# Turning the gated product through VectorE blocks and DRAM instead of TensorE, in nine of eleven FFN steps

## The chip, the cores and the metric

The kernel runs on one core of one Trainium2 chip. The metric is the device time in microseconds of one execution: the median of three runs. The profile shows one further execution, with the engines PE (TensorE), DVE (VectorE), ACT (ScalarE), POOL (GpSimd) and SP (SyncE, which only issues transfers here).

## The reference, cut to what matters

The program is a chain of two transformer blocks on 256 rows of width 1024, in float32. Six times in it stands a gated feed-forward network (FFN) of inner width 2816, and it is the FFN that the change touches:

```
def swiglu_ffn(h, w1, w3, w2):
    return (jax.nn.silu(h @ w1) * (h @ w3)) @ w2
...
        h = h + FFN_RES_WEIGHT * swiglu_ffn(rmsnorm(h, ffn_norm1[i]), ffn1_w1[i], ffn1_w3[i], ffn1_w2[i])
```

Between the FFNs stand a convolution, a latent attention (mla) and a mixer with two more attentions; these are not changed. A projection of a conditioning vector, `mod = silu(c) @ w_mod + b_mod`, is worked out beside the FFNs, in pieces.

## The kernel before, in words

The 256 rows are two row tiles t = 0 and 1 of 128 rows. An FFN runs over NF = 11 steps j of 256 inner columns. The input stands transposed in `x[t]`, split into a high part `xh` and a low part `xl`; each product is three matmuls (high·high, high·low, low·high), the function `mm3`.

In a step, `load(j)` brings three units of 1 MB through SP's queue into a ring of four `raw` buffers: two for w1 and w3 (`up`), one for w2 (`down_in`). ACT casts each 128x512 piece into `whi` (line 82) and DVE makes the rest `wlo` (line 83): 12 pieces a step. `whi`/`wlo` hold 16 pieces for w1 and w3, which is two steps, and 8 for w2. `gu(j, t)` is 24 matmuls of 128x512 into a PSUM bank `wk` (four banks); `gate(j, t)` then makes SiLU on ACT (`sg`, line 340) and the gated product on DVE (`gg`, line 342). `turn(j, t)` transposes `gg` by two PE transposes against an identity (line 106) into PSUM and splits the result into `gh` (ACT, line 82) and `gl` (DVE, line 83). `down(j, t)` is 12 matmuls of `gh`, `gl` with w2 into two banks `acc`.

In the middle steps the code stands in the order load(j), gu(j,0), gu(j,1), then for each tile down(j-1,t), turn(j,t). So a step is 72 matmuls of 128x512 and four transposes. Every engine takes its instructions in one fixed order, which a scheduler writes at build time; an instruction that waits holds up all behind it on its engine. For the part where `pinned` is set, PE keeps the order of the code.

In every second middle step of the first five FFNs, three or four times in each, `mid` calls `mod_group`: two units of w_mod of 1 MB are summed with the conditioning vector in eight DVE instructions into `macc` (lines 992 and 996), two matmuls add over partitions, and a row `mrow` of 512 elements is loaded (line 1006), added to and written to DRAM.

The convolution already sends data through DRAM with POOL's transfers: `land` (line 580) issues four transfers, each of 32 partitions with 8 runs of 624 bytes.

Of the kernel before, what the change touches and what calls it, by code (L numbers as in the profile page):

```python
# [10 lines left out]
F32 = mybir.dt.float32  # L11
F32R = mybir.dt.float32r
# [7 lines left out]
P = 128  # L20
# [11 lines left out]
class Build:  # L32
# [284 lines left out]

    def ffn(self, w, finish, after, mid=None, slow=False, begun=None):
        nc, tc = self.nc, self.tc
        with tc.tile_pool(name=f"ffn{self.n}", bufs=1) as fp:  # L320
            self.fp = fp
            acc = [[self.bank(tag="acc") for _ in range(2)] for _ in range(2)]
            g, w2 = {}, {}

            u = {}

            def up(j):
                u[j] = [self.unit(w[3 * j + i]) for i in range(2)]

            def down_in(j):  # L330
                w2[j] = self.unit(w[3 * j + 2], pool=fp)

            def load(j):
                up(j)
                down_in(j)

            def gate(j, t, ps):
                sc = 1.0 if self.rs[t] is None else self.rs[t][:, :1]
                sg = self.t([P, 256], tag="sg", bufs=2, pool=fp)
                nc.scalar.activation(sg, ps[:, :256], AF.Silu, scale=sc)  # L340
                g[j, t] = self.t([P, 256], tag="gg", bufs=3, pool=fp)
                nc.vector.scalar_tensor_tensor(  # L342
                    out=g[j, t], in0=ps[:, 256:], scalar=sc, in1=sg, op0=ALU.mult, op1=ALU.mult
                )

            def gu(j, t):
                gate(j, t, self.cols(t, u[j], 512))

            def turn(j, t):
                hi = self.t([P, 2, P], F32R, tag=f"gh{t}", bufs=2, pool=fp)  # L350
                lo = self.t([P, 2, P], F32R, tag=f"gl{t}", bufs=2, pool=fp)
                self.transposed(g[j, t], 2, hi, lo)
                g[j, t] = hi, lo

            def down(j, t):
                self.rows(acc[t], g[j, t], w2[j], j == 0, j == NF - 1)

            if begun:
                u[0] = begun[0]
                for t in range(2):  # L360
                    gate(0, t, begun[1][t])
                with self.in_turn():
                    up(1)
                turn(0, 0)
                gu(1, 0)
                down_in(0)
                turn(0, 1)
                gu(1, 1)
                turn(1, 0)
                down_in(1)  # L370
            else:
                load(0)
                load(1)
                gu(0, 0)
                gu(1, 0)
                self.flush()
                turn(0, 0)
                gu(0, 1)
                turn(1, 0)
                gu(1, 1)  # L380
                turn(0, 1)
            down(0, 0)
            turn(1, 1)
            down(0, 1)
            self.pinned = False
            for j in range(2, NF - 1):
                load(j)
                gu(j, 0)
                gu(j, 1)
                if mid:  # L390
                    mid(j)
                for t in range(2):
                    down(j - 1, t)
                    turn(j, t)
            j = NF - 1
            load(j)
            gu(j, 0)
            down(j - 1, 0)
            turn(j, 0)
            ps = self.cols(1, u[j], 512, ks=range(4))  # L400
            down(j, 0)
            finish(0, acc[0])
            post = after(0)
            gate(j, 1, self.cols(1, u[j], 512, ps, range(4, 8)))
            down(j - 1, 1)
            turn(j, 1)
            if not slow:
                post()
            down(j, 1)
            finish(1, acc[1])  # L410
            self.pending.append(after(1))
            if slow:
                post()

    def out_rows(self, x, units, finish, after, mid=None):


        acc, done, post = {}, [0, 0], []

        def step(order):  # L420
            for c in order:
                if c in "pm":
                    (post[0] if c == "p" else mid)()
                    continue
                t = int(c)
                if t not in acc:
                    acc[t] = [self.bank(tag="acc") for _ in range(2)]
                i = done[t]
                z = tuple(v[:, 2 * i : 2 * i + 2] for v in x[t])
                self.rows(acc[t], z, units[i], i == 0, i == 3)  # L430
                done[t] += 1
                if i == 3:
                    finish(t, acc[t])
                    (self.pending if t else post).append(after(t))

        return step
# [544 lines left out]
    def mod_group(self, i):  # L981

        nc, a = self.nc, self.a
        part, which, cols = i // 6, i % 6 // 2, slice(i % 2 * 512, i % 2 * 512 + 512)
        acc = self.t([P, 512], tag="macc", pool=self.fp)
        for u in range(2):
            r = self.raw(a["wmod"][2 * i + u])
            for k in range(4):
                w = r[:, k * 512 : k * 512 + 512]
                s = self.cact[:, 4 * u + k : 4 * u + k + 1]  # L990
                if u == k == 0:
                    nc.vector.tensor_scalar(
                        out=acc, in0=w, scalar1=s, scalar2=None, op0=ALU.mult
                    )
                else:
                    nc.vector.scalar_tensor_tensor(  # L996
                        out=acc, in0=w, scalar=s, in1=acc, op0=ALU.mult, op1=ALU.add
                    )
        hi = self.t([P, 512], F32R, tag="mhi", pool=self.fp)
        lo = self.t([P, 512], F32R, tag="mlo", pool=self.fp)  # L1000
        self.split(hi, lo, acc)
        ps = self.bank()
        self.matmul(ps, self.onesr, hi, start=True, stop=False)
        self.matmul(ps, self.onesr, lo, start=False, stop=True)
        row = self.t([1, 512], tag="mrow", pool=self.fp)
        nc.sync.dma_start(out=row, in_=a["b_mod_2"][0:1, i * 512 : i * 512 + 512])
        nc.vector.tensor_add(row, ps[:1, :], row)
        if which == 1:
            name = ("norm_ffn1_2", "norm_mix_2", "norm_ffn2_2")[part]
            grow = self.t([P, 512], tag="junk")[:1]  # L1010
            nc.sync.dma_start(out=grow, in_=a[name][0:1, cols])
            nc.vector.scalar_tensor_tensor(
                out=row, in0=row, scalar=1.0, in1=grow,
                op0=ALU.add, op1=ALU.mult,
            )
        elif which == 2:
            nc.vector.tensor_scalar(
                out=row, in0=row, scalar1=0.5, scalar2=None, op0=ALU.mult
            )
        nc.sync.dma_start(out=self.mods[i], in_=row)  # L1020
# [553 lines left out]
```

## Time and profile before

| | |
|---|---|
| median of three runs | 1542.34 us (1540.28 to 1542.95) |
| the profiled execution, its own time | 1545.36 us |
| its span from first to last instruction | 1543.2 us |
| PE, DVE, ACT, POOL busy | 98%, 71%, 54%, 4% of the span |
| granted TensorE clock, mean | 0.994 |

Busy shares are means over all stages. The profiled execution is 3.0 us above the median of the runs and 2.2 us above its own span. Matmuls overlap in the records, so their pitch is read from their start times and not from their durations.

### The profile page before, as it was taken

To read this page: it belongs to the slowest core of one execution; us is meant where nothing else is said; L and a number is where in the kernel's file an instruction comes from. 1 tells how busy PE (TensorE), PEld (TensorE's weight loads), DVE (VectorE), ACT (ScalarE), POOL (GpSimd) and SP (SyncE) were. 2 spreads that over 40 slices of the span, in tenths; PEclk is the share of its full clock that TensorE was granted. 3 is DMA by queue.
4 is the path that set the end of the run, shared out by engine and by line. 5 is a ranking of instruction groups with operands and counts; after the bars stand their busy time and mean duration, and the time that the engine had idled before them with its cause. 6 is when DMAs were issued, how large, how long until landed. Compare 5 with 4: busy or idle time off the path is not lost.

```text
span 1543.2 us, 21250 instructions
## 1 busy us (share of the span) xinstructions
PE 1515.7 (98%) x7824; PEld 1239.0 (80%) x7824; DVE 1093.6 (71%) x2136; ACT 830.2 (54%) x1723; POOL 54.6 (4%) x84
## 2 busy tenths in 40 slices
PE   8999997999999999999999999999999999999998
PEld 6888886888888888888788888788888877878886
DVE  7977566587765887658589755888657886975552
ACT  7555454565545555546475544545545565665541
POOL 0000013000000000000000000100001100000000
PEclk9999999999999999999999999999999999999999
DMA  8886479177764676644268754487552543565530
GB/s 307 304 295 254 168 263 254 52 282 270 255 238 149 240 265 232 236 137 143 104 214 310 265 186 176 151 304 273 190 190 97 173 157 120 196 240 189 193 109 28
DMA packets 54923, 316.68 MB, mean 205 GB/s; under 512 B 9210, under 2 KB 12026, under 8 KB 19108
## 3 DMA queue, kind: packets, MB, share of 16 engines
q1 hardware_dynamic: 50596, 308.92, 55.4%
q0 software_dynamic: 2048, 5.11, 1.4%
q10 hardware_dynamic: 2176, 1.30, 0.3%
q8 instruction: 61, 1.00, 0.2%
q14 instruction: 42, 0.34, 0.1%
HBM read 312.93 MB, written 2.39 MB: 204 GB/s over the span
## 4 chain that ended last, share of the span: by engine, by line
PE 91%; DVE 4%; issue 2%; DMA 1%; POOL 1%; ACT 1%; SPq 0%; POOLq 0%; DVEq 0%; ACTq 0%
PE wk L103 52%; PE acc L103 35%; PE wk L106 4%; DVE wlo L83 1%; DMA shifted<-shift 1%; POOL sm L130 1%; DMA h<-in_x_dram 0%; DVE sm L1195 0%; DVE y L259 0%; DVE h L1038 0%; DVE y L1037 0%; ACT pb L1207 0%; DVE pb L1248 0%; DVE pb L1244 0%; DVE y L744 0%
## 5 line engine op out<-in xcount | busy, mean ns | idle before, releaser
L83 DVE TENSOR_TENSOR wlo<-raw,whi 128x512 fp32r<-128x512 f32 x996 | 652.1, 684 | 58.8 <-ACT whi L82 57.0
L82 ACT CAST whi<-raw 128x512 fp32r<-128x512 f32 x996 | 587.5, 619 | 95.0 <-DMA raw<-in_f_dram 27.7
L103 PE MATMUL wk<-whi,xh 128*128 128x512 f32 x1120 | 443.8, 396 | 0.5
L103 PE MATMUL wk<-wlo,xh 128*128 128x512 f32 x1120 | 437.5, 391 | 0.2 <-DVE wlo L83 0.2
L103 PE MATMUL wk<-whi,xl 128*128 128x512 f32 x1120 | 437.6, 391 | 0.0
L103 PEld LDWEIGHTS wk<-whi,xl 128*128 128x128 f32 x1120 | 210.8, 188 | 44.9
L103 PEld LDWEIGHTS wk<-whi,xh 128*128 128x128 f32 x1120 | 211.0, 188 | 43.5 <-ACT xh L85 1.5
L103 PEld LDWEIGHTS wk<-wlo,xh 128*128 128x128 f32 x1120 | 211.2, 189 | 42.8 <-DVE wlo L83 0.6
L103 PE MATMUL acc<-whi,gh 128*128 128x512 f32 x528 | 212.2, 402 | 1.0 <-ACT gh L82 0.9
L103 PE MATMUL acc<-whi,gl 128*128 128x512 f32 x528 | 207.3, 393 | 0.0
L103 PE MATMUL acc<-wlo,gh 128*128 128x512 f32 x528 | 206.7, 392 | 0.0
L340 ACT ACTIVATE sg<-wk,sm 128x256 f32<-128x256 f32 x88 | 41.7, 474 | 195.5 <-PE wk L103 194.1
L342 DVE SCALAR_TENSOR_TENSOR gg<-wk,sm,sg 128x256 f32<-128x256 f32 x88 | 42.4, 481 | 110.0 <-ACT sg L340 108.6
L103 PE MATMUL acc<-whi,xh 128*128 128x512 f32 (+2 forms) x304 | 117.9, 388 | 0.7 <-ACT xh L82 0.7
L103 PEld LDWEIGHTS acc<-whi,gl 128*128 128x128 f32 x528 | 99.1, 188 | 21.7
L103 PEld LDWEIGHTS acc<-whi,gh 128*128 128x128 f32 x528 | 99.3, 188 | 21.4 <-ACT gh L82 2.1
L103 PE MATMUL acc<-wlo,xh 128*128 128x512 f32 (+2 forms) x304 | 116.1, 382 | 0.0
L103 PE MATMUL acc<-whi,xl 128*128 128x512 f32 (+2 forms) x304 | 115.7, 382 | 0.0
L103 PEld LDWEIGHTS acc<-wlo,gh 128*128 128x128 f32 x528 | 99.4, 188 | 19.9
L82 ACT CAST gh<-wk 128x256 fp32r<-128x256 f32 x132 | 48.8, 370 | 120.6 <-PE wk L106 120.5
L83 DVE TENSOR_TENSOR gl<-wk,gh 128x256 fp32r<-128x256 f32 x132 | 55.4, 420 | 64.1 <-ACT gh L82 64.0
L996 DVE SCALAR_TENSOR_TENSOR macc<-raw,cact,macc 128x512 f32<-128x512 f32 x126 | 94.4, 749 | 2.8
(279 smaller groups left out, 1179.1 us busy)
## 6 DMA issues: line engine op xcount, KB each, us to landing
raw<-in_f_dram SPq DMA_DIRECT2D x196, 1024.0 KB
raw<-in_wmod_dram SPq DMA_DIRECT2D x36, 1024.0 KB
raw<-in_win_dram SPq DMA_DIRECT2D x16, 1024.0 KB
raw<-in_pw_dram SPq DMA_DIRECT2D x12, 1024.0 KB
shifted<-shift POOLq DMA_DIRECT2D x32, 156.0 KB, 6.3
raw<-in_wo_dram SPq DMA_DIRECT2D x4, 1024.0 KB
raw<-in_wbr_dram SPq DMA_DIRECT2D x4, 1024.0 KB
raw<-in_wout_dram SPq DMA_DIRECT2D x4, 1024.0 KB
```

The costliest lines, as they stand in the source:

```text
L82: i = nc.scalar.copy(hi, src)
L83: j = nc.vector.tensor_tensor(out=lo, in0=src, in1=hi.bitcast(F32), op=ALU.subtract)
L103: return self.pin(self.nc.tensor.matmul(*args, **kw))
L106: return self.pin(self.nc.tensor.transpose(out, src, ident))
L130: self.nc.gpsimd.tensor_tensor(out=r, in0=v, in1=self.mhalf[:, :1].to_broadcast([P, w]), op=ALU.pow)
L340: nc.scalar.activation(sg, ps[:, :256], AF.Silu, scale=sc)
L342: nc.vector.scalar_tensor_tensor(out=g[j, t], in0=ps[:, 256:], scalar=sc, in1=sg, op0=ALU.mult, op1=ALU.mult)
L996: nc.vector.scalar_tensor_tensor(out=acc, in0=w, scalar=s, in1=acc, op0=ALU.mult, op1=ALU.add)
```

## The change

`turn` remains in step 0 and in step 10. In steps 1 to 9 it is replaced by `move(j, t)` behind the gate, and by `back(j, t)` where `turn` stood. `move` has DVE transpose `gg` within 32x32 blocks into `gb`, and POOL issue four transfers (32 partitions, 8 runs of 128 bytes each) into a DRAM tile of its own. `back` has POOL issue one transfer (128 partitions, 2 runs of 512 bytes each) into `gt`, which is split into `gh` and `gl` as before, now out of SBUF. `gg` has two buffers and not three. The row of `mod_group` now lies in the first partition of `macc`, so that the load of the bias waits until `macc` has been split. In FFNs that don't begin the program, w1 and w3 of steps 0 and 1 are loaded ahead of both w2 units. PE is pinned in the last step.

```diff
-                g[j, t] = self.t([P, 256], tag="gg", bufs=3, pool=fp)
+                g[j, t] = self.t([P, 256], tag="gg", bufs=2, pool=fp)
...
+            def move(j, t):
...
+                b = self.t([P, 8, 32], tag="gb", bufs=2, pool=fp)
+                nc.vector.transpose(b.rearrange("p b s -> p (b s)"), g[j, t])
+                g[j, t] = d = dram.tile([2, P, P], F32, name=f"{name}_{j}_{t}")
+                to = d.rearrange("k (c f) (a s) -> a f (k c) s", f=32, s=32)
+                for a in range(4):
+                    nc.gpsimd.dma_start(out=to[a], in_=b[32 * a : 32 * a + 32])
+
+            def back(j, t):
+                r = self.t([P, 2, P], tag="gt", bufs=2, pool=fp)
+                nc.gpsimd.dma_start(out=r, in_=g[j, t].rearrange("k p s -> p k s"))
+                g[j, t] = parts(t)
+                self.split(*g[j, t], r)
...
-                load(0)
-                load(1)
+                up(0)
+                up(1)
                 gu(0, 0)
                 gu(1, 0)
+                move(1, 0)
                 self.flush()
                 turn(0, 0)
                 gu(0, 1)
-                turn(1, 0)
+                down_in(0)
                 gu(1, 1)
+                move(1, 1)
                 turn(0, 1)
-            down(0, 0)
-            turn(1, 1)
-            down(0, 1)
+                down_in(1)
+            for t in range(2):
+                down(0, t)
+                back(1, t)
             self.pinned = False
             for j in range(2, NF - 1):
                 load(j)
-                gu(j, 0)
-                gu(j, 1)
+                for t in range(2):
+                    gu(j, t)
+                    move(j, t)
                 if mid:
                     mid(j)
                 for t in range(2):
                     down(j - 1, t)
-                    turn(j, t)
+                    back(j, t)
+            self.pinned = True
...
-        row = self.t([1, 512], tag="mrow", pool=self.fp)
+        row = acc[:1]
```

In the changed file the lines are others: `sg` is line 345, `gg` 347, the block transpose 368, the writes 372, the read 376, the sums into `macc` 1024 and 1028, the bias row 1039.

On ACT, in a middle step of the last FFN, the rows from `sg` of tile 1 to `sg` of tile 0 of the next step were these (`wk` behind `gh` is the PSUM bank of PE's transposes; the three further casts of the w2 unit between the last two `whi` rows shown and `gh` are left out):

```order
L340 ACTIVATE sg_14879<-wk_14854 128x256
L82 CAST whi_15103<-raw_15089 128x512
L82 CAST gh_3751_14895<-wk_14897 128x256
L82 CAST whi_14959<-raw_14957 128x512
...
L82 CAST gh_3754_14914<-wk_14916 128x256
L340 ACTIVATE sg_15000<-wk_14975 128x256
```

Now they are these, at the same places:

```order
L345 ACTIVATE sg_15485<-wk_15460 128x256
L82 CAST whi_15726<-raw_15712 128x512
L82 CAST gh_3836_15510<-gt_15508 128x256
L82 CAST whi_15570<-raw_15568 128x512
...
L82 CAST gh_3839_15528<-gt_15526 128x256
L345 ACTIVATE sg_15611<-wk_15586 128x256
```

No row has moved; both `gh` now read `gt`, which POOL's read fills, and `sg` of the next step still stands behind the second of them.

On DVE, in a step of the third FFN that runs a `mod_group` (`gl` reads `gt`; `macc` is the sum of `mod_group`), from `gg` of tile 1 to `gg` of tile 0 of the next step and its block transpose:

```order
L347 SCALAR_TENSOR_TENSOR gg_6293<-wk_6266,sm_1274_5495,sg_6291 128x256
L1039 TENSOR_TENSOR macc_6302<-wk_6319,macc_6302 1x512
L368 STREAM_TRANSPOSE gb_6295<-gg_6293 128x256
...
L83 TENSOR_TENSOR gl_1497_6343<-gt_6340,gh_1496_6342 128x256
...
L83 TENSOR_TENSOR gl_1500_6361<-gt_6358,gh_1499_6360 128x256
L1028 SCALAR_TENSOR_TENSOR macc_6652<-raw_6659,cact_274,macc_6652 128x512 x2
L347 SCALAR_TENSOR_TENSOR gg_6445<-wk_6418,sm_1259_5407,sg_6443 128x256
L1028 SCALAR_TENSOR_TENSOR macc_6652<-raw_6659,cact_274,macc_6652 128x512
L368 STREAM_TRANSPOSE gb_6447<-gg_6445 128x256
```

The block transposes are new in DVE's queue, behind the bias row; two sums of `macc` stand behind the second `gl`, and one ahead of the next block transpose.

On POOL, which issued nothing in the FFNs before, two steps near the end of the program now read (`ffn_8_0` is the DRAM tile of step 8, row tile 0):

```order
L372 DMA ffn_8_0_15779<-gb_15777 32x8x32 x4
L376 DMA gt_15832<-ffn_8_0_15779 128x2x128
L372 DMA ffn_8_1_15815<-gb_15813 32x8x32 x4
L376 DMA gt_15850<-ffn_8_1_15815 128x2x128
L372 DMA ffn_9_0_15941<-gb_15939 32x8x32 x4
L376 DMA gt_15994<-ffn_9_0_15941 128x2x128
```

Each read stands right behind the writes of its own tile, and ahead of the writes of the next tile.

## Rows read from the trace of the kernel before

**Rows 1.** The page: span, PE's share, granted clock and DMA share in 40 slices.

```profile
PE 1515.7 (98%) x7824; PEld 1239.0 (80%) x7824; DVE 1093.6 (71%) x2136; ACT 830.2 (54%) x1723; POOL 54.6 (4%) x84
...
PEclk9999999999999999999999999999999999999999
DMA  8886479177764676644268754487552543565530
```

**Rows 2.** Timeline of PE around one pair of transposes: start us, us, engine, line, operation.

```profile
72.36 0.39 PE L103 MATMUL acc<-whi,gl 128*128 128x512 f32 x1
72.59 0.38 PE L106 MATMUL wk<-ident,gg 128*128 128x128 f32 x2
72.73 0.48 PE L103 MATMUL acc<-whi,gh 128*128 128x512 f32 x1
73.05 0.40 PE L103 MATMUL acc<-wlo,gh 128*128 128x512 f32 x1
```

**Rows 3.** Timeline of PE, last FFN: first and last of 32 matmuls in a row.

```profile
1451.23 0.39 PE L103 MATMUL wk<-wlo,xh 128*128 128x512 f32 x1
...
1458.26 0.39 PE L103 MATMUL wk<-whi,xl 128*128 128x512 f32 x1
```

**Rows 4.** Timeline of ACT, one step of the last FFN; idle time before, and releaser.

```profile
1453.25 0.38 ACT L340 ACTIVATE sg<-wk 128x256 f32<-128x256 f32 x1 [4.80 <-PE wk L103]
1453.93 4.70 ACT L82 CAST whi<-raw 128x512 fp32r<-128x512 f32 x7 [0.30 <-PE wk L103]
1458.69 0.39 ACT L340 ACTIVATE sg<-wk 128x256 f32<-128x256 f32 x1
1461.68 0.37 ACT L82 CAST gh<-wk 128x256 fp32r<-128x256 f32 x1 [2.10 <-PE wk L106]
1464.98 0.37 ACT L82 CAST gh<-wk 128x256 fp32r<-128x256 f32 x1
1470.15 0.38 ACT L340 ACTIVATE sg<-wk 128x256 f32<-128x256 f32 x1 [4.80 <-PE wk L103]
```

**Rows 5.** Timeline of DVE in the same step.

```profile
1459.27 0.42 DVE L342 SCALAR_TENSOR_TENSOR gg<-wk,sg 128x256 f32<-128x256 f32 x1
1459.61 0.69 DVE L83 TENSOR_TENSOR wlo<-raw,whi 128x512 fp32r<-128x512 f32 x1
1465.72 0.42 DVE L83 TENSOR_TENSOR gl<-wk,gh 128x256 fp32r<-128x256 f32 x1
```

**Rows 6.** Timeline of DVE, two steps of the second FFN with a mod_group.

```profile
385.01 0.48 DVE L342 SCALAR_TENSOR_TENSOR gg<-wk,sm,sg 128x256 f32<-128x256 f32 x1
385.40 0.67 DVE L1007 TENSOR_TENSOR mrow<-wk,mrow 1x512 f32<-1x512 f32 x1
391.18 0.75 DVE L996 SCALAR_TENSOR_TENSOR macc<-raw,cact,macc 128x512 f32<-128x512 f32 x1
396.80 0.48 DVE L342 SCALAR_TENSOR_TENSOR gg<-wk,sm,sg 128x256 f32<-128x256 f32 x1
402.80 0.48 DVE L342 SCALAR_TENSOR_TENSOR gg<-wk,sm,sg 128x256 f32<-128x256 f32 x1
```

**Rows 7.** The tile `shifted`: POOL's 32 transfers, and their time to landing.

```profile
L580 POOL DMA_DIRECT2D shifted<-shift x32: 583/583/762, 217.2 to 271.0; - x32
...
DMA to landing us min/median/max: 3.3/6.3/10.8
```

**Rows 8.** The same tile, 256 to 261 us: eight transfers beside a weight load.

```profile
DMA to landing us min/median/max: 8.6/10.4/10.8
```

**Rows 9.** The same tile, 269 to 272 us: four transfers, nothing else under way.

```profile
DMA to landing us min/median/max: 3.5/3.7/3.9
```

**Rows 10.** DMA queues, 214 to 272 us (58 us): packets, MB, share of 16 engines.

```profile
q0 software_dynamic: 1917, 4.82, 35.6%
q10 hardware_dynamic: 2176, 1.30, 9.1%
```

**Rows 11.** Windows of FFNs 2, 4 and 6: the last three columns are PEclk, DMA share, GB/s.

```profile
310.00:495.00 185.00, 184.87 (x838) 152.11 (x837) 136.45 (x235) 99.26 (x194) 1.42 (x2) 1.00 0.66 240
790.00:980.00 190.00, 188.92 (x854) 154.22 (x853) 137.26 (x265) 102.78 (x197) 2.41 (x3) 1.00 0.60 219
1352.00:1541.00 189.00, 184.93 (x831) 150.37 (x830) 104.53 (x177) 86.97 (x163) 0.94 (x1) 1.00 0.42 152
```

More of the change, by code (lines that the diff above doesn't have):

```diff
@@ L319, in ffn @@
         nc, tc = self.nc, self.tc
-        with tc.tile_pool(name=f"ffn{self.n}", bufs=1) as fp:
+        with ExitStack() as ctx:
+            name = f"ffn{self.n}"
+            fp = ctx.enter_context(tc.tile_pool(name=name, bufs=1))
+            dram = ctx.enter_context(
+                tc.tile_pool(name=name + "d", bufs=1, space=bass.MemoryType.DRAM)
+            )
             self.fp = fp
@@ L347, in gu, with parts @@
                 gate(j, t, self.cols(t, u[j], 512))
+            def parts(t):
+                return tuple(
+                    self.t([P, 2, P], F32R, tag=f"{n}{t}", bufs=2, pool=fp) for n in ("gh", "gl")
+                )
             def turn(j, t):
[L350 to L353, printed above, removed]
+                pair = parts(t)
+                self.transposed(g[j, t], 2, *pair)
+                g[j, t] = pair
+            def move(j, t):
[10 more added lines that the diff above has]
+                self.split(*g[j, t], r)
             def down(j, t):
@@ L368, in ffn @@
                 gu(1, 1)
-                turn(1, 0)
+                move(1, 1)
                 down_in(1)
             else:
-                load(0)
-                load(1)
+                up(0)
+                up(1)
                 gu(0, 0)
                 gu(1, 0)
+                move(1, 0)
                 self.flush()
@@ L378, in ffn @@
                 gu(0, 1)
-                turn(1, 0)
+                down_in(0)
                 gu(1, 1)
+                move(1, 1)
                 turn(0, 1)
-            down(0, 0)
-            turn(1, 1)
-            down(0, 1)
+                down_in(1)
+            for t in range(2):
+                down(0, t)
+                back(1, t)
             self.pinned = False
@@ L413, in ffn @@
                 post()
+            self.pinned = False
     def out_rows(self, x, units, finish, after, mid=None):
```

## The prediction, made blind

> **What bounds the kernel now.** I read the page first: PE is busy 98% of the span at full clock; DVE (71%), ACT (54%) and the transfers (mostly under nine tenths) have room [rows 1]. So whatever leaves PE's queue shortens the program, if nothing else comes to hold PE up. Then the timelines of one step of the last FFN, which has no `mod_group` and repeats cleanly. On PE, 32 matmuls start within 7.03 us, a pitch of 7.03 / 31 = 0.227 us [rows 3]; a step of 72 is 16.34 us. On ACT, `sg` of tile 0 comes every 1470.15 - 1453.25 = 16.90 us, each time after 4.8 us of waiting for PE [rows 4]. PE sets the pace, and ACT's 4.8 us is the slack that this change draws on.
>
> **What is removed.** 108 pairs of transposes (9 steps, 2 tiles, 6 FFNs). From the matmul ahead of a pair to the second one behind it 0.69 us pass, against two pitches, 0.45 us: 0.24 us a pair [rows 2], 0.48 us a step. The step itself gives 16.90 - 16.34 = 0.56 us [rows 3, 4]. With 0.5 us a step, 54 steps give **27 us** (26 to 30). It is a gain only where PE waits for nothing new.
>
> **What is added, and where it waits.** Each tile now goes gg, block transpose, four writes, one read, `gh`, `gl`. PE needs `gh` and `gl` only after two more gates, a step and a half later, so PE itself would hardly notice. But the order of ACT and DVE has not moved: `gh` of tile 1 still stands just ahead of the next step's `sg`, and `gl` ahead of the next `gg`. If the data are late there, the next gate is late, the next tile's writes start late, and the loop sg, 7 casts, sg, round trip, gh can become longer than PE's step.
>
> So I compare two times in the last FFN. PE finishes the next gate's matmuls at 1453.25 + 16.34 = 1469.59; `gh` (0.37 us) has to start by 1469.2 [rows 4]. `sg` of tile 1 starts at 1458.69, `gg` follows at 1459.27, one `wlo` ends at 1460.30 [rows 4, 5]. The block transpose is in no row: the nearest DVE rows of 128x256 take 0.42 us [rows 5]; between 0.2 and 0.7 us (a 128x512 piece) I take 0.42. With 0.1 us for each hand-over POOL issues at 1460.8. **The round trip R, from the first write's issue to the read's landing, may therefore last 8.4 us.**
>
> What R will be: POOL needs 0.583 us for a transfer of 256 runs [rows 7], and both new kinds have 256 runs, so the fourth write is issued 1.75 us after the first. Then come one landing of a write and one of the read, and 0.2 us for two waits. No row has a POOL transfer that writes DRAM; `shifted` (POOL, as many runs, out of DRAM) landed in 3.3 us at the shortest, 3.5 to 3.9 with nothing else under way, 6.3 in the median, and 8.6 to 10.8 beside a weight load [rows 7 to 9]. Thus R is 1.95 + 2 x 3.3 = 8.55 us at the short end and 1.95 + 2 x 6.3 = 14.55 at the median. The engines are busy 0.42 of the time in the last FFN, 0.60 to 0.66 in others [rows 11]. Sharing between 3.3 and 6.3 by that, less 0.4 us because 128-byte runs carry a fifth of the data, gives 4.2 and 4.8 us. I take the middle between that and 3.3, 3.75 and 4.05, since three weight loads of a step start together when buffers come free and leave gaps: **R = 9.45 us in the last FFN, 10.05 in the others**.
>
> The Trainium skill, "DMA: Bandwidth & Descriptors", section "Specifications", speaks against short runs: under 512 bytes the engine reads, modifies and writes. No row here shows this for a write of 128 bytes; the sum goes by the rows above and the rows on price per run below.
>
> **The overrun of a step.** Last FFN: 9.45 - 8.4 = 1.05 us. In FFNs with `mod_group` DVE has more in the loop. From `gg` of tile 1 to the next `gg` there were 396.80 - 385.01 = 11.8 us, 11.3 without transposes [rows 6]. Now gg, mrow, block transpose, hand-over, R, gh, gl and one to two sums of 0.75 stand there: 3.3 to 4.0 us beside R, so R may last about 7.6 us. In the next step a sum and `mlo` stand between the two gates, which takes 6.0 us (402.80 - 396.80), 0.6 more than PE's 24 matmuls; a limit of 8.4 less 0.6 is 7.8. Mean 7.7 to 7.8: overrun 10.05 - 7.8 = 2.25 us.
>
> **The sum.** Overruns add up from step 1 to 9. PE first absorbs them, but in step 10 `turn(10,0)` needs a gate that stands behind `gl` of step 9, so PE pays all but what it can do meanwhile, `down(9,0)` of 12 x 0.227 = 2.7 us less 0.5 for `gg`: 2.2 us. Last FFN: 9 x 1.05 - 2.2 = 7.3. FFNs 2 to 5: 9 x 2.25 - 2.2 = 18 each, 72 in all. In the first FFN up to step 6 the second `gl` has more weight pieces ahead of it; I halve: 9. At the start of FFNs 2 to 5 `gl` of DRAM tile (1,0) stands ahead of `gl` of (0,1), which `down(0,1)` waits for, and in FFNs 2 to 4 one `down` matmul moves ahead of its w2 cast: 5 (0 to 20). Together +93.5 - 27 = +66 on the profiled 1545.4, so 1612; less 3.0, as the runs' median stands to it, **1610**.
>
> Costed at nothing: POOL's issues, 10 x 0.583 = 5.8 us of a step; the wait of a read behind its writes holds the next tile's writes, which are ready only 5.4 us later, so up to 2 us in a busy case, inside the range. The bias row's load on SP now waits for `macc` to be split; behind it stand weight loads about a step ahead of use, 1.3 us late, covered by that step. `gg` with two buffers is free again after the block transpose. The pinned last step keeps PE's order but for eight transposes at two FFN ends, under 1 us each.
>
> **Rivals.**
> *Hidden (0.20).* The landings come near the short end. At 3.3 us R is 8.55: nothing in the last FFN, 9 x 0.75 - 2.2 = 4.6 in FFNs 2 to 5, 2 in the first: 1545.4 - 27 + 20 - 3 = 1535. Shorter, with R under 7.8, all 27 us stay: 1515. It decides at R = 8.7, a landing of about 3.4 us. For it: a write is 32 KB, not 156. Against: 3.5 with nothing under way. The Trainium skill's fit in "DMA: Bandwidth & Descriptors", "Anatomy of one DMA — SWDGE (gpsimd) path", about 2.0 us and a small part by bytes, gives by estimate R = 6.4 us and the 1515; the trace's shortest landing, 3.3 us, speaks against it.
> *Busy queue (0.12).* Landings at the median, R = 14.55: 9 x 6.15 - 2.2 = 53 in the last FFN, 9 x 6.75 - 2.2 = 58.6 in four, 29 in the first, 10 at starts: 1545.4 - 27 + 326 - 3 = 1842. I count from 1740 here.
> *The transfer engines become the bound (0.06).* POOL's 4.82 MB are 7724 runs of 624 bytes, which took 0.356 x 16 x 58 us / 7724 = 43 ns each; writes of 636 bytes (q10) took 39 ns a packet [rows 10]; runs of 128 bytes lie between a fifth, 9 ns, and 43. A step's 2048 writes and 512 reads (of 43 ns) are then 2.5 to 6.9 us on each of 16 engines, 0.15 to 0.42 of a step beside 0.60 to 0.66 [rows 11]. At the upper end loads come late by some 0.08 x 16.3 = 1.3 us a step, 45 steps: 1542 - 27 + 60 = 1575.
> *No difference (0.04).* R within 0.1 us of 8.7: gain and overruns cancel.
> *Overruns of 0.5 to 4 us a step (0.58).* The forecast; 1560 to 1690 is its own range.
>
> **How the numbers follow.** A change under 0.2% (3 us) can't be told from none. Hidden is faster, 0.20; no difference 0.04; the other three are slower, 0.76. The range 1526 to 1740 leaves out the fully hidden case, about 0.08, and the busy queue, 0.12.
>
> **What would show it.** Right: the pitch between `sg` of tile 0 in the last FFN above 16.4 us, at 17 to 18, and more in FFNs 2 to 5; ACT waiting for the read of `gt` ahead of `gh` instead of for PE ahead of `sg`; PE waiting for `gh` or `gl` late in each FFN; PE's share at 93 to 96%. Wrong: ACT still waiting for PE ahead of `sg`, and a step of 16.3 us (hidden); `raw` as the releaser of casts (transfer engines). The clock I leave at its full level: it stood at nine tenths or more in every slice, the convolution with its waits too [rows 1].

## The result, and the profile after

The changed kernel takes 1663.62 us (median of 4 runs, 1661.22 to 1665.53); the kernel before took 1541.84 us beside it. The ratio is 1.0788 (95% interval 1.0775 to 1.08): slower by 122 us. The profiled execution has a span of 1660.1 us; before it was 1543.2.

From the page of the changed kernel, the busy times, the granted clock in 40 slices, and the chain of work that ended last by engine and by line, as in [rows 1]:

```profile
PE 1540.4 (93%) x7608; PEld 1240.9 (75%) x7608; DVE 1103.9 (66%) x2244; ACT 789.9 (48%) x1723; POOL 385.7 (23%) x624
...
PEclk9999999999999999989999999999999999999999
...
PE 35%; DMA 33%; DVE 13%; POOL 8%; issue 6%; ACT 4%; POOLq 0%; SPq 0%; DVEq 0%; ACTq 0%
PE acc L103 18%; DMA gt<-ffn 16%; PE wk L103 15%; DMA ffn<-gb 15%; POOL ffn L372 6%; DVE wlo L83 3%; DVE macc L1028 2%; PE wk L106 2%; ACT whi L82 2%; ACT gh L82 1%; DMA raw<-in_f_dram 1%; DVE gb L368 1%; DVE gl L83 1%; DVE gg L347 1%; POOL gt L376 1%
```

Before, the chain by engine was:

```profile
PE 91%; DVE 4%; issue 2%; DMA 1%; POOL 1%; ACT 1%; SPq 0%; POOLq 0%; DVEq 0%; ACTq 0%
```

PE has fewer instructions in a longer span: 98% has become 93%. A third of the chain that ended last is now landings of DMA, and by line these are the read `gt<-ffn` and the writes `ffn<-gb`, with POOL's issues of the writes behind them. The waits say the same (engine and line, what it waited for, us in total, times, the longest):

```profile
ACT gh L82 <- DMA gt<-ffn: 524.0, 107, 10.3
DVE gl L83 <- ACT gh L82: 382.7, 110, 8.2
POOL ffn L372 <- DVE gb L368: 314.6, 55, 10.1
POOL gt L376 <- DMA ffn<-gb: 256.1, 69, 6.6
...
ACT sg L345 <- PE wk L103: 37.8, 15, 7.9
```

ACT waited for the data ahead of 107 of its 108 casts `gh`, and hardly ever for PE ahead of `sg`; before, each `sg` of tile 0 came after 4.8 us of waiting for PE [rows 4]. PE no longer sets the pace. Times of the new operations (ns: shortest, median, longest; at the end us from issue to landing), from the views of the tiles `gt` and `gb`:

```profile
L376 POOL DMA_DIRECT2D gt<-ffn x108: 712/717/728, 38.6 to 1636.2; - x108
...
DMA to landing us min/median/max: 2.4/3.7/7.2
```

```profile
L372 POOL DMA_DIRECT2D ffn<-gb x432: 582/582/824, 31.4 to 1633.7; - x144
L368 DVE STREAM_TRANSPOSE gb<-gg x108: 421/440/448, 30.6 to 1627.8; 128x256 f32<-128x256 f32 x108
```

A step of the second FFN shows how the time passes. POOL, then ACT, then DVE in the same stretch (start, duration, instruction, and in brackets its idle time before and what ended it):

```profile
396.48 2.32 POOL L372 DMA_DIRECT2D ffn<-gb  x4 [7.11 <-DVE gb L368]
404.25 0.72 POOL L376 DMA_DIRECT2D gt<-ffn  x1 [5.46 <-DMA ffn<-gb]
404.96 2.32 POOL L372 DMA_DIRECT2D ffn<-gb  x4
410.17 0.72 POOL L376 DMA_DIRECT2D gt<-ffn  x1 [2.88 <-ACT whi L82]
```

```profile
391.49 0.41 ACT L82 CAST gh<-gt 128x256 fp32r<-128x256 f32 x1 [2.14 <-DMA gt<-ffn]
391.80 0.47 ACT L345 ACTIVATE sg<-wk,sm 128x256 f32<-128x256 f32 x1
...
398.94 0.47 ACT L345 ACTIVATE sg<-wk,sm 128x256 f32<-128x256 f32 x1
399.31 3.22 ACT L82 CAST whi<-raw 128x512 fp32r<-128x512 f32 x6
408.88 0.41 ACT L82 CAST gh<-gt 128x256 fp32r<-128x256 f32 x1 [6.36 <-DMA gt<-ffn]
...
412.77 0.40 ACT L82 CAST gh<-gt 128x256 fp32r<-128x256 f32 x1 [2.43 <-DMA gt<-ffn]
413.08 0.47 ACT L345 ACTIVATE sg<-wk,sm 128x256 f32<-128x256 f32 x1
```

```profile
394.69 0.48 DVE L347 SCALAR_TENSOR_TENSOR gg<-wk,sm,sg 128x256 f32<-128x256 f32 x1
395.09 0.74 DVE L1028 SCALAR_TENSOR_TENSOR macc<-raw,cact,macc 128x512 f32<-128x512 f32 x1
395.75 0.44 DVE L368 STREAM_TRANSPOSE gb<-gg 128x256 f32<-128x256 f32 x1
...
400.91 0.44 DVE L368 STREAM_TRANSPOSE gb<-gg 128x256 f32<-128x256 f32 x1
```

Read it as a ring. `gh` of tile 1 at 391.49 lets `sg` go at 391.80; `gg` follows at 394.69 and `gb` at 395.75, with sums of `macc` ahead of each on DVE; POOL writes tile 0 from 396.48; its read, the next row on the queue, is issued when the writes have landed, at 404.25. Tile 1's `gb` was ready at 400.91 + 0.44 = 401.35, but its writes stand behind that read and start at 404.96, held for 3.6 us. They land, the read goes at 410.17, and `gh` of tile 1 runs at 412.77, 21.3 us after the last one. PE's work for the step is 16.34 us [rows 3]. (The last bracket on POOL names ACT. By the trace the last of tile 1's writes had landed 0.56 us before that read, and the last of tile 0's 0.61 us before the read at 404.25, so I take the landing as what released both.)

The means over steps 2 to 9 of FFNs 2 to 5 (32 steps), worked out from the starts and ends of the same rows in each step, are, around the ring: 2.56 us from `gh` to the end of `gb`, 0.34 to the first write, 2.35 for four issues, 3.61 until the read is issued, 0.71 to tile 1's first write, 2.35 for four issues, 3.98 until its read, 0.72 for that issue and 2.82 to `gh`. The pieces follow on each other, so they must add up to the step, 19.43 us; what they show is that 10.4 us of it are waits for landings and 6.1 us POOL's issues. Tile 1's writes were held for 1.5 us in the mean, and for over 0.5 us in 32 of 32 steps.

Is PE in this ring at all? The 37.8 us that `sg` waited for PE lie, but for 1.1 us, ahead of step 2 or in step 10 of an FFN. In steps 2 to 9 of all six FFNs PE held up ACT or DVE between `gh` of tile 1 and the next `gb` once, for 2.9 us.

### The profile page after: what moved, and what is told of

It is laid out like the page before. It is cut to its first block, busy times and chain, and to the rows that moved or that the text cites. A ratio compares the mean times of both kernels' runs of the same rounds, so it can differ in the third digit from the quotient of the medians.

```text
span 1660.1 us, 22050 instructions
## 1 busy us (share of the span) xinstructions
PE 1540.4 (93%) x7608; PEld 1240.9 (75%) x7608; DVE 1103.9 (66%) x2244; ACT 789.9 (48%) x1723; POOL 385.7 (23%) x624
## 4 chain that ended last, share of the span: by engine, by line
PE 35%; DMA 33%; DVE 13%; POOL 8%; issue 6%; ACT 4%; POOLq 0%; SPq 0%; DVEq 0%; ACTq 0%
PE acc L103 18%; DMA gt<-ffn 16%; PE wk L103 15%; DMA ffn<-gb 15%; POOL ffn L372 6%; DVE wlo L83 3%; DVE macc L1028 2%; PE wk L106 2%; ACT whi L82 2%; ACT gh L82 1%; DMA raw<-in_f_dram 1%; DVE gb L368 1%; DVE gl L83 1%; DVE gg L347 1%; POOL gt L376 1%
## 5 line engine op out<-in xcount | busy, mean ns | idle before, releaser
L83 DVE TENSOR_TENSOR wlo<-raw,whi 128x512 fp32r<-128x512 f32 x996 | 628.6, 679 | 25.5 <-ACT whi L82 20.9
L82 ACT CAST whi<-raw 128x512 fp32r<-128x512 f32 x996 | 555.2, 616 | 77.7 <-PE acc L103 30.5
L372 POOL DMA_DIRECT2D ffn<-gb x432 | 251.2, 588 | 378.8 <-DVE gb L368 314.6
L103 PE MATMUL acc<-whi,gh 128*128 128x512 f32 x528 | 226.7, 429 | 82.2 <-ACT gh L82 82.1
L82 ACT CAST gh<-gt 128x256 fp32r<-128x256 f32 x108 | 43.8, 406 | 524.0 <-DMA gt<-ffn 524.0
L83 DVE TENSOR_TENSOR gl<-gt,gh 128x256 fp32r<-128x256 f32 x108 | 45.9, 425 | 369.1 <-ACT gh L82 369.1
L103 PE MATMUL acc<-whi,gl 128*128 128x512 f32 x528 | 222.3, 421 | 6.9 <-DVE gl L83 6.9
L103 PE MATMUL acc<-wlo,gh 128*128 128x512 f32 x528 | 221.4, 419 | 0.0
L376 POOL DMA_DIRECT2D gt<-ffn x108 | 77.5, 718 | 396.4 <-DMA ffn<-gb 256.1
L130 POOL TENSOR_TENSOR sm<-sm,mhalf 128x1 f32<-128x1 f32 (+3 forms) x36 | 36.2, 1006 | 405.4 <-DVE sm L152 243.1
```

The source lines that it names most:

```text
L82: i = nc.scalar.copy(hi, src)
L83: j = nc.vector.tensor_tensor(out=lo, in0=src, in1=hi.bitcast(F32), op=ALU.subtract)
L103: return self.pin(self.nc.tensor.matmul(*args, **kw))
L130: self.nc.gpsimd.tensor_tensor(out=r, in0=v, in1=self.mhalf[:, :1].to_broadcast([P, w]), op=ALU.pow)
L372: nc.gpsimd.dma_start(out=to[a], in_=b[32 * a : 32 * a + 32])
L376: nc.gpsimd.dma_start(out=r, in_=g[j, t].rearrange("k p s -> p k s"))
```

## The experiments

Times are medians, ratios are against the kernel before, timed beside each. Line numbers are those of each kernel. Dots mark lines of an edit that are not shown.

**1. late.** The split into `gh` and `gl` is queued behind the next step's first gate:

```diff
 def back(j, t):
-    g[j, t] = parts(t)
-    self.split(*g[j, t], r)
+    g[j, t] = r
+def late(j, t, at):
+    r, g[j, t] = g[j, t], parts(t)
+    with tc.issue_after(gates[at][0].ins), tc.issue_after(gates[at][1].ins):
+        self.split(*g[j, t], r)
...
     gu(j, t)
     move(j, t)
+    if t == 0:
+        late(j - 1, 0, (j, 0))
+        late(j - 1, 1, (j, 0))
...
```

> Same operations and transfers as the changed kernel; only the place of the split into gh and gl moves: it is queued on ScalarE and VectorE behind sg and gg of tile 0 of the next step, instead of ahead of them. Theory 1 (the gates of the next step stand behind casts that wait for the round trip through DRAM): the waits of gh and gl for gt all but vanish, the step of an FFN comes down to about 16.3 us, the time to 1515 to 1525 us, below both kernels. Theory 2 (the traffic of the 540 small transfers slows TensorE's loads or the weights' transfers): the transfers are the same, so most of the 122 us stays, 1600 us or more. Theory 3 (the granted clock, which was 0.968 over the span against 0.994): if the clock falls for a reason other than TensorE's waits, it stays near 0.968 and the time does not come below about 1550 us.

1576.94 us, ratio 1.0223 [1.0196, 1.0251], clock 0.985. Most of the loss is gone (87 of 122 us), but the size expected by theory 1 was missed: ACT still stood 327.4 us before `gh`.

```profile
ACT gh L82 <- DMA gt<-ffn: 327.4, 53, 11.0
```

Both casts now stand ahead of tile 1's gate, and tile 1's data, held behind tile 0's on POOL, come still later than that place. Theory 2 falls here already: the transfers are all there.

**2. traffic.** All transfers stay, nobody uses them:

```diff
...
-    g[j, t] = d = dram.tile(...)
+    sent[j, t] = d = dram.tile(...)
...
     nc.gpsimd.dma_start(out=r, in_=sent[j, t]...)
-    g[j, t] = parts(t)
-    self.split(*g[j, t], r)
+    turn(j, t)
```

> The product goes through TensorE as in the kernel before (three buffers for it), while VectorE's block transpose, the four writes and the read into gt of each row tile are still issued; what they bring is not used. Theory 1: nothing waits for the round trip, so the time is that of the kernel before plus at most 9 x 5 x 2 x 0.44 us of block transposes, if all of them lay on the path: 1540 to 1560 us. Theory 2: near the changed kernel's 1664 us, above 1600.

1545.83 us, ratio 1.0026 [1.0016, 1.0037].

**3. rest.** `move` does nothing and `back` is `turn`; only the order of loads, the bias row and the pinned step remain of the change (`gg` has three buffers again).

```diff
 def move(j, t):
-    b = self.t([P, 8, 32], tag="gb", bufs=2, pool=fp)
...
+    pass
 def back(j, t):
-    r = self.t([P, 2, P], tag="gt", bufs=2, pool=fp)
...
+    turn(j, t)
```

> Only the other edits of the change: the order of the weights' loads at an FFN's start and end, the bias row in another tile, the pinned last step; the product goes through TensorE in every step and nothing through DRAM. Theory 1: within 5 us of the kernel before, 1537 to 1547 us. The rival that these edits cost a part of the 122 us: above 1550 us.

1545.2 us, ratio 1.0022 [1.0011, 1.0032]: 0.22% of 1541.3, 3.4 us, for the edits that are not the product's way. Between rest and traffic there are 0.6 us, inside both intervals: 540 transfers on POOL's queue and 108 block transposes cost nothing that can be measured when nobody waits for them.

**4. one.** One write for each tile, in the order in which it lies:

```diff
-    to = d.rearrange("k (c f) (a s) -> a f (k c) s", f=32, s=32)
-    for a in range(4):
-        nc.gpsimd.dma_start(out=to[a], in_=b[32 * a : 32 * a + 32])
+    to = d.rearrange("k p s -> (k p s)").rearrange("(r b s) -> r b s", r=P, s=32)
+    nc.gpsimd.dma_start(out=to, in_=b)
```

> Each row tile is written to DRAM by one transfer of 128 rows of 1 KB instead of four of 32 rows, so that the values of the product land permuted; everything behind it is as in the changed kernel. Three issues of 0.58 us fall out of the round trip, 1.75 us. Theory 1: the steps that wait for the round trip (9 in each of the first five FFNs) become shorter by about 1.75 us each, 79 us, and the clock recovers a part: 1575 to 1600 us. Theory 2, by volume (the bytes are the same): no change, 1650 us or more.

1599.8 us, ratio 1.0387 [1.0364, 1.0411]: 64 us faster than the changed kernel, at the upper edge of what was expected (79 us, by 1.75 us in each of 45 steps). Other instructions moved with it (the casts among them), so the size is not the issues' alone.

**5. late2.** As late, but each tile's split stands behind the gate of the same tile:

```diff
-    if t == 0:
-        late(j - 1, 0, (j, 0))
-        late(j - 1, 1, (j, 0))
+    late(j - 1, t, (j, t))
...
```

> As the run late, but the split of tile 1 is queued behind the gate of tile 1 of the next step instead of tile 0's. In late ScalarE still waited 327 us for gt, in single waits of up to 11.0 us, because the round trip of tile 1 (12.9 us from gg to the end of the read in one step of the second FFN) is longer than the way from its gate to the next step's first. With one gate more, some 5 to 6 us, theory 1 expects that nearly all of these waits go: steps of 16.3 us, 1515 to 1530 us. If something else than the place of the split kept late at 1577 us (the transfers beside the weights, the clock), the time stays above 1555 us.

1528.86 us, ratio 0.9911 [0.9878, 0.9944]: 13 us under the kernel before, an interval clear of 1, and 135 us under the changed kernel, with the same transfers. The waits of late2:

```profile
ACT sg L345 <- PE wk L103: 287.1, 77, 7.9
...
POOL gt L376 <- DMA ffn<-gb: 219.3, 51, 6.4
```

POOL waits for the landings as before, but ACT is back to waiting for PE ahead of `sg`. A step on ACT reads:

```profile
387.85 0.48 ACT L345 ACTIVATE sg<-wk,sm 128x256 f32<-128x256 f32 x1 [4.82 <-PE wk L103]
388.22 0.40 ACT L82 CAST gh<-gt 128x256 fp32r<-128x256 f32 x1
...
394.44 0.47 ACT L345 ACTIVATE sg<-wk,sm 128x256 f32<-128x256 f32 x1
394.81 0.39 ACT L82 CAST gh<-gt 128x256 fp32r<-128x256 f32 x1
...
404.23 0.47 ACT L345 ACTIVATE sg<-wk,sm 128x256 f32<-128x256 f32 x1 [4.85 <-PE wk L103]
```

`gh` follows `sg` and waits for nothing; 404.23 - 387.85 = 16.38 us, which is PE's step.

**6. wfirst.** On POOL, both tiles' writes ahead of both reads:

```diff
...
+    with tc.issue_after(wrote[j, 1].ins):
         nc.gpsimd.dma_start(out=r, in_=g[j, t].rearrange("k p s -> p k s"))
```

> The changed kernel with one thing moved on GpSimd's queue: the four writes of tile 1 stand ahead of the read of tile 0, so that they don't stand behind a read that waits for the writes of tile 0 to land. Everything else is as in the changed kernel. Theory 1b (a part of the round trip of tile 1 is that its writes are held on GpSimd: 3.5 us in one step of the second FFN): 1 to 2.5 us off 45 steps, 1560 to 1620 us. If only the landings make the round trip, no change: 1650 to 1670 us; above that if the read of tile 0, now behind tile 1's gate, is what PE then waits for.

1638.11 us, ratio 1.0628 [1.0613, 1.0644]: 25.5 us off, and so inside neither range that was named: below the 1650 to 1670 us of no change, above theory 1b's 1560 to 1620. POOL in wfirst:

```profile
394.54 2.34 POOL L372 DMA_DIRECT2D ffn<-gb  x4 [8.75 <-DVE gb L368]
399.71 2.31 POOL L372 DMA_DIRECT2D ffn<-gb  x4 [2.83 <-DVE gb L368]
402.33 0.72 POOL L377 DMA_DIRECT2D gt<-ffn  x1 [0.30 <-issue]
407.53 0.71 POOL L377 DMA_DIRECT2D gt<-ffn  x1 [4.49 <-DMA ffn<-gb]
```

Tile 1's writes now start when `gb` is there. What is gained so is partly lost again: from tile 1's last write to its read 4.77 us pass in the mean over the 32 steps, 3.98 in the changed kernel. The step is 18.71 us instead of 19.43, 0.72 x 45 = 32 us by this sum against the 25.5 measured.

**7. eight**, four extra writes to a tile `e` ahead of the real ones.

```diff
-    for a in range(4):
-        nc.gpsimd.dma_start(out=to[a], in_=b[32 * a : 32 * a + 32])
...
+    for o in (e, d):
+        to = o.rearrange("k (c f) (a s) -> a f (k c) s", f=32, s=32)
+        for a in range(4):
+            nc.gpsimd.dma_start(out=to[a], in_=b[32 * a : 32 * a + 32])
```

> Four more writes of the same kind, to a second DRAM tile that nothing reads, are issued ahead of the four real ones. Theory 1: the round trip grows by four issues of 0.58 us, 2.33 us, and 45 waiting steps by as much, the last FFN by 9 x 2.33 - 2.2 = 19 us: +105 to +125 us, 1770 to 1790 us. Theory 2 (traffic alone): the run traffic cost 4.5 us with all transfers in it, so half as much again would be 2 us: 1666 us.

1656.98 us, ratio 1.075 [1.0704, 1.0797]. Neither theory's number: the extra issues moved other instructions. In steps 2 to 9 of all FFNs tile 1's writes stand ahead of tile 0's read, as in wfirst, and the next step's gate of tile 0 ahead of `gh` of tile 1, as in late. It tests nothing alone.

**8. pin8**, the same with the changed kernel's order held fast for gates, `gh`, writes and reads:

```diff
+    with tc.issue_after(done[j - 1][0].ins) if j > 1 and t == 0 else ExitStack():
         nc.scalar.activation(sg, ...)
...
+    with tc.issue_after(gt[j, 0][1].ins) if t else ExitStack():
...
+    if not t:
+        read(j, t)
```

> The run eight again with the changed kernel's order held fast, since there the extra writes moved other instructions: in eight the writes of tile 1 stood ahead of the read of tile 0, and in a part of the steps sg stood ahead of gh, as in the runs wfirst and late. Here sg and gg of a step's tile 0 stand behind gh and gl of the step before, and tile 1's writes behind tile 0's read, as in the changed kernel. Theory 1: the round trip of one tile grows by four issues, 2.33 us, and where tile 1's writes wait behind tile 0's read by eight, 4.66 us: 45 steps give +105 to +210 us, 1770 to 1870 us. If issues on GpSimd are hidden in the landings: within 20 us of 1664.

1927.01 us, ratio 1.2492 [1.246, 1.2525]: +263 us, 57 us above the upper end. A step on POOL, `ffn779e` being the extra tile:

```profile
472.45 2.32 POOL L377 DMA_DIRECT2D ffn779e<-gb  x4 [4.85 <-DVE gb L370]
474.76 2.50 POOL L377 DMA_DIRECT2D ffn<-gb  x4
481.58 0.72 POOL L390 DMA_DIRECT2D gt<-ffn  x1 [4.32 <-ACT whi L82]
482.29 2.32 POOL L377 DMA_DIRECT2D ffn779e<-gb  x4
484.60 1.73 POOL L377 DMA_DIRECT2D ffn<-gb  x3
486.87 0.58 POOL L377 DMA_DIRECT2D ffn<-gb  x1 [0.54 <-DMA gt<-ffn]
491.31 0.72 POOL L390 DMA_DIRECT2D gt<-ffn  x1 [3.86 <-DMA ffn<-gb]
```

None of the second tile's writes is issued before the first tile's read. The mean step of FFNs 2 to 5 is 23.90 us, 4.47 above the changed kernel's, which is two times four issues (4.66); 45 steps make 201 us. The last FFN, which had been nearly at PE's pace, took 223.5 us from its first to its last gate instead of 175.6, another 48. So both tiles' issues count, nearly in full: the ring goes through both. The size is not as clean as the sign, since casts, sums and loads had changed places here too, and no run holds this order without the extra writes.

**9. warm and 10. warm4.** Matmuls of zeros where PE waits, ten in warm and four in warm4:

```diff
...
+    with tc.issue_after(self.mm.ins):
+        for _ in range(10):
+            self.mm = nc.tensor.matmul(acc[0][0], self.zeros[:, :P], self.zeros, start=False, stop=False)
...
```

The zeros also have a buffer of their own in both.

> Ahead of the first down matmul of each step from 2 to 9, where TensorE waits for gh, ten matmuls of zeros are added to the accumulator (they change no value): 480 of 0.21 us, 102 us of work that fits into the waits, which are some 4 us a step. Theory 1 (the round trip sets the step and the fall of the granted clock to its half level is only its consequence): the clock recovers, the time stays within 15 us of 1664. Theory 3 (the half clock costs a part of its own: (0.994 - 0.968) x 1660 = 43 us at most): the clock recovers to about 0.99 and the time falls to 1620 to 1640 us.

> As the run warm, with four matmuls of zeros a step instead of ten: 192 of 0.21 us, 41 us of work in the waits. In warm the granted clock recovered from 0.968 to 0.987 and the time still rose by 25 us; ten matmuls a step may have cost more than the clock gave back. If the half clock costs time of its own, up to 30 us (149 matmuls more than before started in stretches of half clock, 0.2 us longer each), four a step should show it: 1635 to 1655 us with a clock above 0.975. If its fall only follows the waits: 1660 to 1680 us, in proportion to warm.

warm: 1688.21 us, ratio 1.0959 [1.0941, 1.0977]; warm4: 1685.03 us, 1.0919 [1.0881, 1.0956]. Both lie above every range that was named. Span and mean granted clock of the changed kernel, of warm and of warm4, in this order:

```profile
core 0: 1660.1 us, clock 0.968
```

```profile
core 0: 1683.3 us, clock 0.987
```

```profile
core 0: 1685.1 us, clock 0.970
```

No gain in either, whatever the clock did. The waits that the matmuls were to fill were smaller than the expectation's "some 4 us a step". PE's waits ahead of `down` for `gh`, in the changed kernel and in warm:

```profile
PE acc L103 <- ACT gh L82: 82.1, 39, 4.5
```

```profile
PE acc L103 <- ACT gh L82: 33.0, 23, 3.9
```

82.1 us are at most 1.7 in each of the 48 steps, and ten matmuls take 2.1. But warm4 rose nearly as much as warm with less than half the work, so the rise isn't the added matmuls' time alone; in both, loads on SP and casts had changed places too. The runs show no price of the clock, and don't measure it either.

**11. bare.** No turning at all; `gh` and `gl` come straight from `gg`.

```diff
...
 def back(j, t):
-    r = self.t([P, 2, P], tag="gt", bufs=2, pool=fp)
-    nc.gpsimd.dma_start(out=r, in_=g[j, t].rearrange("k p s -> p k s"))
+    r = g[j, t].rearrange("p (k s) -> p k s", k=2)
```

> The product is neither turned on TensorE nor sent through DRAM in the nine steps: gh and gl are split straight from gg (three buffers), so the values stand in the wrong places; everything else is as in the changed kernel. It shows alone what taking the 108 pairs of transposes from TensorE is worth. By the prediction's term of 0.5 us in each of 54 steps: 27 us below the run rest (1545), 1515 to 1520 us. If the pairs were mostly hidden behind something else: above 1530 us.

1518.51 us, ratio 0.9852 [0.9837, 0.9867], as the prediction's term says. ACT waits for PE ahead of `sg` again:

```profile
ACT sg L345 <- PE wk L103: 303.1, 79, 8.0
```

**12. best.** late2 with the loads at the start as before, and the last step not pinned.

```diff
-    up(0)
-    up(1)
+    load(0)
+    load(1)
...
-    self.pinned = True
     j = NF - 1
```

> The run late2 (split of each tile behind the gate of the same tile of the next step) with the loads at an FFN's start in the order of the kernel before and the last step not pinned. The run rest, with these edits and PE's transposes, came out 3.4 us above the kernel before. If those edits cost that, 3 to 4 us below late2's 1528.9: 1523 to 1527 us; if they are noise or needed by the rest: 1525 to 1533 us.

1527.17 us, ratio 0.9914 [0.9883, 0.9946], not to be told from late2, and inside the second range, 0.2 us past the first; one of its six executions took 1542.25. That the 3.4 us of rest come back this way is not shown.

## Why the prediction came out as it did

The sign and the mechanism were right; the time was 54 us short, inside the range. Of the signs named beforehand, PE's share (93%), ACT's waits for `gt` and PE's for `gh` came. Against bare, where `gh` waits for no transfer, every stage can be priced: us from the start of the first `gg` row of an FFN on DVE to that of its last.

| FFN | before | bare | changed | late2 | loss, changed - bare | predicted loss |
|---|---|---|---|---|---|---|
| 1 | 173.8 | 169.0 | 201.4 | 169.9 | 32.4 | 9 |
| 2 to 5 | 705.7 | 693.6 | 798.7 | 696.6 | 105.1 | 72 + 5 |
| 6 | 170.8 | 169.4 | 175.6 | 169.4 | 6.2 | 7.3 |
| sum | | | | | 143.7 | 93.3 |

The sum is nearly the difference of the spans, 1660.1 - 1515.3 = 144.8.

*What is removed, 27 us.* Right: rest less bare is 1545.2 - 1518.5 = 26.7 us.

*In which order things stand.* Right. late and late2 edit nothing but the place of the split (the scheduler then put some casts and loads elsewhere too), and 87 and 135 us go with it; traffic keeps all of the transfers and nearly nothing of the loss. The rival of the transfer engines falls with that.

*The round trip R.* Right in size: 10.05 us predicted with `mod_group`; measured, from the first write's issue to the read's landing, 9.8 for tile 1 and 10.3 for tile 0 in FFNs 2 to 5. The landings were near the 4.05 chosen from the rows of `shifted` [rows 7]: medians of 3.7, neither the hidden case's 3.3 nor the busy queue's 6.3. The Trainium skill's fit in "DMA: Bandwidth & Descriptors", "Anatomy of one DMA — SWDGE (gpsimd) path", 2.0 us and a part by bytes, gives by estimate 2.3 us for the read: near its shortest landing here, 2.4, and 1.4 us under the median.

*The overrun of a step, 2.25 us: the step that failed.* It set one R against the time between two gates, as if each tile's trip began at its own gate, and put "the wait of a read behind its writes holds the next tile's writes" among what costs nothing, up to 2 us in a busy case. In all 32 steps of FFNs 2 to 5 tile 1's writes were held, 1.5 us in the mean, which is 1.2 more than tile 0's; the loop goes through tile 0's trip and then tile 1's. Its length, 19.43 us, is 3.1 above PE's 16.34. The prediction's own sum with the hold put in, 9.8 + 1.2 - 7.75 = 3.3 us, comes near that. pin8 speaks for both tiles' issues counting, and wfirst's order, which takes the hold away, gave back some 25 us.

*The first FFN, halved to 9.* Wrong: 32.4. Its steps 2 to 9 took 20.1 us in the mean, no less than the mean of FFNs 2 to 5; if the further `wlo` pieces ahead of `gl` gave cover, it doesn't show.

*The starts, 5 (0 to 20).* Too small, but inside its range. From an FFN's third gate to its fifth, which is the first of step 2, the changed kernel took 24.0, 18.5, 25.1, 20.8, 21.9 and 24.6 us in the six FFNs, bare 15.1 to 17.3. In FFNs 2 to 5 that is 23.6 us more, of which four common overruns of 3.1 are 12.4; some 11 are left for this term.

*The last FFN, +7.3.* The size, 6.2, was right by luck. R was 8.2 us for tile 1, not 9.45, and so under the limit of 8.4: by the prediction's sum nothing would have been lost. Instead the stretch up to step 2 took 24.6 us (bare 15.8), the next steps 16.1 to 18.0, and the last two 14.1 and 13.7 as PE caught up.

*Edits costed at nothing.* 3.4 us (rest); which of them was not tried.

*The clock "at its full level".* Wrong as a statement: it fell to half, 1.2 GHz, in 25 stretches, 106 us of the span, where before there were four, 20 us in all, 10 of them in the convolution, which the means over slices in [rows 1] hide. The window of one of the 25 (busy us and instructions by engine, granted clock, DMA share, GB/s), PE's waits from 703 us to its end, and two of its matmuls:

```profile
711.10:717.90 6.80, 4.70 (x11) 3.73 (x12) 4.69 (x9) 5.16 (x11) 2.32 (x4) 0.50 0.25 69
```

```profile
PE acc L103 <- ACT gh L82: 4.3, 1, 4.3
```

```profile
714.22 0.63 PE L103 MATMUL acc<-whi,gl 128*128 128x512 f32 x1
714.64 0.63 PE L103 MATMUL acc<-whi,gh 128*128 128x512 f32 x1
```

The stretch begins inside a wait of 4.3 us ahead of a `down`. 22 of the 25 lie in FFNs, 21 of these at a wait of PE for `gh` or `gl`. By count of PE's rows 201 matmuls of 128x512 began at half clock, 14 before (the 149 of the run warm4's expectation were counted with the convolution's small matmuls). Their pitch was 0.427 us instead of 0.227 [rows 3], so 187 more are 37 us of PE's time. In steps 2 to 9 PE hardly stands in the ring (see the profile after), so the slow matmuls of those steps lay beside what set the step; what the half clock costs at the starts is not shown. late2, where PE waited 4.3 us in all for `gh`, stands at 0.997.

late2's executions spread from 1520 to 1533 us, bare's from 1517 to 1522; where the 10 us between their medians go was not settled. In late2's profiled one, which was its fastest, the steps are PE's.

## What to carry to other kernels

Work moved off the busiest engine onto a round trip of DMA paid here only where what consumes the result stood, on each in-order queue, behind the next round of work that feeds the trip: the same transfers gave 1.0788 with the cast ahead of the next gate and 0.9911 behind it. Before costing such a trip, walk the whole ring through every queue, the issuing one too: here a read that waited for its own writes held the next tile's writes, and the trips added up instead of overlapping. Shortening the trip (fewer issues, another order of writes) gave back 25 to 64 of 122 us; taking it out of the loop gave back 135.

## What was not expected of the hardware

- POOL takes 0.717 us to issue the read, against 0.582 for a write with as many runs (the views of `gt` and `gb` above).
- In the median a write of 32 KB took as long to land as a read of 128 KB. From the page's part on DMA issues (KB each, median us to landing):

```profile
ffn<-gb POOLq DMA_DIRECT2D x432, 32.0 KB, 3.7
gt<-ffn POOLq DMA_DIRECT2D x108, 128.0 KB, 3.7
```

- 540 small transfers beside the 309 MB of the loads' queue cost 0.6 us (traffic less rest), not to be told from nothing, as long as nobody waited for them.
